# Mixer and mixture-of-experts layer on one core: where each expert's branch count is loaded into a register

## The chip, the cores and the metric

One core of one Trainium2 chip. The metric is the device time of one execution in microseconds (us). The kernel before takes 1189.96 us, the median of 3 runs (1186.68 to 1193.52).

## What is computed

A decoder layer on 256 tokens of width 1024: two kinds of attention, a gated merge and an output projection, and behind them a mixture of 32 experts, of which each token uses four. The change lies in the experts. Cut to them, the reference is:

```python
logits = (hf @ w_router + b_router).astype(jnp.float32)
top_val, top_idx = lax.top_k(logits, TOP_K)
top_w = jax.nn.softmax(top_val, axis=-1)
combine = ...
for e in range(N_EXPERTS):
    gu = hf @ w_gate_up[e] + b_gate_up[e]
    gate = jnp.minimum(gu[:, :D_EXPERT], SWIGLU_LIMIT)
    up = jnp.clip(gu[:, D_EXPERT:], -SWIGLU_LIMIT, SWIGLU_LIMIT)
    act = (up + 1.0) * (gate * jax.nn.sigmoid(SWIGLU_ALPHA * gate))
    y = y + combine[:, e:e + 1] * (act @ w_down[e] + b_down[e])
```

All weights are float32: 8 MiB of gate and up and 4 MiB of down per expert.

## The kernel before

The mixer and the router fill the first 235 us of the span. Then the loop over the experts runs (L1267), one **block** per expert `j`. A block multiplies up to 64 tokens that chose expert `j`, gathered to 64 rows, with the gate and up weights (`up_mm`, L1021, tile `ps_g`), and then does the down product of the expert ahead of it (`down(j - 1)`, L1089, tile `ps_d`), with the transposes of the activation (L1042, `ps_t`) between. Blocks with an odd `j` also add two finished experts to the output (`add_pair`, L1135), and every fourth gathers the tokens of the next four experts (L984).

**Weights.** They arrive in pieces of 2 MiB, four of gate and up and two of down per expert, all issued from the SyncE queue (SP, L78) in a fixed order. Ten slots hold them. `Slots.pump` sends a piece off once the piece that had its slot ten places earlier has been used, which is told by the matmuls that read it. A late block so delays transfers as well.

**Branches.** An expert may have more than 64 tokens. So a block begins, for `j` from 2 to 31, with `more(j)` (L1204): a branch on `arm[j]`, an integer that is over 0 where expert `j` or `j - 1` has tokens beyond 64. Where it is 0, as for nearly all, the body (`more_down`, `more_up`) is jumped over. The branch is on TensorE, VectorE, ScalarE and GpSimd, and each needs the number in a register. `load(arm, j)` (L1177, L1178) puts it there. On TensorE that is three instructions, which the trace calls TENSOR_LOAD, FUSED_REGOPS and SEQ_ASSERT (the first stands as TENSOR_LOAD, the others as ISA in the order of instructions below); they run in the engine's sequencer, which hands the matmuls to the engine. `hint(j + 1)` (L1200) puts a prefetch hint for the next block's branch behind the first matmuls of a block.

`arm` is computed once, in `counts()` (L924), during block 1. Nothing but that ties a load to a place in the program, and the scheduler, which orders each engine's instructions, puts the loads of TensorE into two bunches: 9 at the end of block 1, ahead of the branch of block 2, and 21 at the end of block 2, ahead of the branch of block 3. On VectorE and ScalarE each load stands at its own branch; GpSimd has none of the work here.

Of the kernel before, what the change touches and what calls it, by code (L numbers as in the profile page):

```python
# [100 lines left out]
def hybrid_layer(ctx: ExitStack, tc: tile.TileContext, x, c, w_mod, b_mod, g_pre_mix, g_post_mix,  # L101
# [118 lines left out]
    arm = keep.tile([1, E + 1], I32, name="arm")  # L220
# [9 lines left out]
    state_act = {}  # L230
# [776 lines left out]
    def gu_banks(n=2):  # L1007
        return [psg.tile([128, 512], FT, name="ps_g", tag=f"g{b}") for b in range(n)]

    def up_mm(e, C, xe, release=False, pg=None, ks=range(NK)):  # L1010

        n = 128 // C
        nb = 4 // n
        if pg is None:
            pg = gu_banks(nb)
        for k in ks:
            wt = W.get(i_gu[e][k // 2])
            for b in range(nb):
                for s in range(n):
                    c0 = s * nb * 512 + b * 512  # L1020
                    last = mm(pg[b][s * C:(s + 1) * C, :], xe[:, k, :], wt[:, k % 2, c0:c0 + 512],  # L1021
                              start=(k == 0), stop=(k == NK - 1), skip_group_check=True)
                    if k == ks[0]:
                        state_act["up"] = last
                    state_act["up_end"] = last
            if release and k % 2:
                W.done(i_gu[e][k // 2])
        return pg

    def up_out(pg, b, tag, bufs):  # L1030
        gu = wk.tile([128, 512], FT, name="gu", tag=tag, bufs=bufs)
        if b % 2:
            nc.vector.tensor_copy(gu, pg[b])  # L1033
        else:
            nc.scalar.copy(gu, pg[b])  # L1035
        return gu
# [40 lines left out]
    def down_mm(e, C, act, first=0, release=False, then=None):  # L1077

        nj = C // 8
        if e == E - 1 and first:  # L1080
            pds = gu_banks()
        else:
            pds = [pst.tile([128, 512], FT, name="ps_d", tag="t")] * 2
        for k in range(NK):
            wt = W.get(i_dn[e][k // 4])
            a = act[:, k % nj, (k // nj) * C:(k // nj) * C + C]
            for h in range(2):
                p0 = 64 * (h ^ first)
                mm(pds[h][p0:p0 + C, :], a, wt[:, k % 4, h * 512:(h + 1) * 512],  # L1089
                   start=(k == 0), stop=(k == NK - 1), skip_group_check=True)  # L1090
            if release and k % 4 == 3:
                W.done(i_dn[e][k // 4])
            if then and k % 4 == 3:
                then(k // 4)
        return pds
# [6 lines left out]
    def down(e, release=True, then=None):  # L1102

        pds = down_mm(e, 64, acts[e], e % 2, release, then)
        if e % 2 == 0:
            dns[e // 2] = pairs.tile([128, 2, 2, 512], FR, name="dn2", tag="dn")
        for h in range(2):
            rows = slice(64 * (h ^ (e % 2)), 64 * (h ^ (e % 2)) + 64)
            hi, lo = (dns[e // 2][rows, h, a, :] for a in range(2))
            weight = wsl[e // 2][rows, h:h + 1]  # L1110
            state_act["down"] = nc.scalar.activation(hi, pds[h][rows, :], AF.Copy, scale=weight)  # L1111
            nc.vector.scalar_tensor_tensor(lo, pds[h][rows, :], weight, hi.bitcast(FT), op0=OP.mult, op1=OP.subtract)  # L1112
# [52 lines left out]
    def more_down(e):  # L1165
        s0, C = CHUNKS[0]
        scatter(down_32(e, ov, "guo"), scatter_rows(e, s0, "so", C))

    def more_up(e):
        s0, C = CHUNKS[0]  # L1170
        for bank in gu_banks():
            nc.tensor.transpose(bank[:, :128], ident, ident)
        xo = gather([e], s0, C, "xo")[:, :, 0, :]
        pg = up_mm(e, C, xo, pg=[pst.tile([128, 512], FT, name="ps_go", tag="t")])
        up_act(e, C, 0, up_out(pg, 0, "guo", 1), ov)

    def load(t, j):  # L1177
        return nc.values_load(t[0:1, j:j + 1], engines=ENGINES, min_val=0, max_val=S)  # L1178

    def rest(e, i):  # L1180

        s0, C = CHUNKS[i]
        with tc.If(load(cnt, e) > s0):
            xo = gather([e], s0, C, "xo")[:, :, 0, :]
            pg = [pst.tile([128, 512], FT, name="ps_go", tag="t") for _ in range(C // 32)]
            for half in range(2):
                for q in range(2):
                    W.again(i_gu[e][2 * half + q], free_slots[q])
                up_mm(e, C, xo, False, pg, range(4 * half, 4 * half + 4))
            for q in range(2):  # L1190
                W.again(i_dn[e][q], free_slots[q])
            a = wk.tile([128, C // 8, 64], FT, name="ao", tag="xo")
            for b in range(C // 32):
                up_act(e, C, b, up_out(pg, b, "guo", 1), a)
            st = scatter_rows(e, s0, "so", C)
            scatter(down_64(e, a) if C == 64 else down_32(e, a, "guo"), st)
            if i + 1 < len(CHUNKS):
                rest(e, i + 1)

    def hint(j):  # L1200

        tc.mark_branch_hint_location(f"more{j}", "LikelyTaken", ENGINES[:1])

    def more(j):  # L1204


        with tc.If(load(arm, j) > 0, label=f"more{j}"):  # L1207
            if j - 1 not in FREE:
                with tc.If(load(cnt, j - 1) > 64):
                    more_down(j - 1)  # L1210
            if j < E - 1:
                with tc.If(load(cnt, j) > 64):
                    more_up(j)
            else:
                for bank in gu_banks():
                    nc.tensor.transpose(bank[:, :128], ident, ident)
                with tc.If(load(arm, E) > 0):
                    streamed = dict(W.tiles)
                    for e in range(E):
                        rest(e, int(e not in FREE))  # L1220
                    W.tiles = streamed

    last_slots = [W.items[k][2] for k in i_gu[E - 1]]
    free_slots = [W.items[k][2] for k in i_dn[E - 3]]
    quads, gus, acts, sts, wsl, dns = {}, {}, {}, {}, {}, {}

    def gather_quad(j, between=None):
        quads[j // 4] = gather([j, j + 1, j + 2, j + 3], 0, 64, "xe", between)

    def activate(j, b):  # L1230
        if b == 0:
            acts[j] = wk.tile([128, 8, 64], FT, name="act", tag="act", bufs=2)
        up_act(j, 64, b, gus[j][b], acts[j])
# [3 lines left out]
    def before_last():  # L1237

        add_pair((E - 4) // 2)
        scatter_pair(E - 2)  # L1240
# [26 lines left out]
    for j in range(E):  # L1267
        if j == 0:
            gather_quad(0, first_up)
        elif j not in FREE or j == E - 1:  # L1270
            if j == E - 1:
                before_last()
            more(j)
        xe = quads[j // 4][:, :, j % 4, :]
        if j == 0:
            pg = up_mm(0, 64, xe, True, pgs, range(NK - 2, NK))
        elif 1 < j < E - 1:
            pg = up_mm(j, 64, xe, True)
        elif j > 1:
            pg = up_mm(j, 64, xe, True, None, range(NK - 2))  # L1280
            with tc.issue_after(state_act["up_end"].ins):
                gate_row()
            up_mm(j, 64, xe, True, pg, range(NK - 2, NK))
        else:
            pg = gu_banks()
            for b, ks in enumerate((range(0, 4), range(4, 6), range(6, NK))):
                up_mm(1, 64, xe, True, pg, ks)
                if b < 2:
                    with tc.issue_after(state_act["up_end"].ins):
                        activate(0, b)  # L1290
        gus[j] = [up_out(pg, b, "gu", 2) for b in range(2)]
        if 0 < j < E - 1:
            with tc.issue_after(state_act["up"].ins):
                hint(j + 1)
        if j % 2 and 3 <= j < E - 1:
            with tc.issue_after(state_act["up_end"].ins):
                add_pair((j - 3) // 2)
        if j % 4 == 3 and j < E - 1:
            gather_quad(j + 1)
        if j == E - 1:  # L1300
            residual()
        if j == 0:
            weights()
        if j == 1:
            with tc.issue_after(state_act["up_end"].ins):
                counts()
                scatter_bias()
        if j % 2 and j < E - 1:
            scatter_pair(j - 1)
        if j:  # L1310
            down(j - 1, then=lambda b: activate(j, b))
    with tc.issue_after(state_act["down"].ins), tc.issue_after(state_act["sig"].ins):
        nc.scalar.preload_act_table_set(EXP_LN)
    down(E - 1)
# [44 lines left out]
```

## Time and profile before

| what | value |
|---|---|
| median of 3 runs | 1189.96 us |
| the profiled execution's own time | 1186.46 us |
| its span in the trace | 1184.7 us |
| TensorE matmul busy (PE) | 1060.4 us, 90% |
| TensorE weight load busy (PEld) | 536.6 us, 45% |
| VectorE (DVE), ScalarE (ACT), GpSimd (POOL) busy | 37%, 21%, 2% |
| moved by DMA | 461.60 MB, mean 390 GB/s |
| granted TensorE clock, mean | 0.973 |

The span is the time from the first to the last instruction; 1.8 us of the execution lie around it. The profiled execution is faster than all three timed runs, by 3.5 us than their median. "Idle before" a matmul tells what released it: `PEq L1207` is TensorE's own sequencer at the branch of `more`. A busy TensorE alone doesn't tell what sets the pace, since an engine that is fed at the pace of the transfers can look nearly as busy.

### The profile page before, as it was taken

Reading aid. Unit: us, or ns where it says so; the run is one execution under the profiler, and the core shown is the slowest. Engines: PE = TensorE matmul, PEld = TensorE weight load, DVE = VectorE, ACT = ScalarE, POOL = GpSimd, SP = SyncE. Lnnn points to the kernel's source line nnn. Section 1 sums busy time; section 2 is a strip of 40 time slices with the busy share of each in tenths; the row PEclk is TensorE's granted clock in tenths of the full one; section 3 lists DMA queues with packets and bytes.
Section 4 is the critical chain, followed back from the end, with each engine's and each line's share of the span. In section 5 each row is a group of like instructions: output and inputs, shape, how many; then the busy total and the mean of one; then the engine's idle time right before and its main releaser. Section 6 shows DMA issues by size and latency. Waiting matters only on the chain. (4 is left out here: it accounts for less than half of the span.)

```text
span 1184.7 us, 14417 instructions
## 1 busy us (share of the span) xinstructions
PE 1060.4 (90%) x5662; PEld 536.6 (45%) x5662; DVE 443.8 (37%) x963; ACT 248.2 (21%) x472; POOL 24.0 (2%) x39
## 2 busy tenths in 40 slices
PE   5999999898778999998999999899888988898886
PEld 4987999632233434344434343344323332333232
DVE  3586978614212333222323332223222322232234
ACT  3455674511000111011111111011001100010023
POOL 2022000000000000000000000000000000000000
PEclk9999999988989999997999999999999999999998
DMA  9988796979978999999999999999999999999993
GB/s 326 392 307 320 280 333 250 387 297 403 380 326 349 426 427 426 426 427 428 428 426 427 425 425 429 425 428 423 427 427 425 429 425 426 425 428 425 428 421 153
DMA packets 51902, 461.60 MB, mean 390 GB/s; under 512 B 4117, under 2 KB 4234, under 8 KB 27210
## 3 DMA queue, kind: packets, MB, share of 16 engines
q1 hardware_dynamic: 50992, 458.77, 93.7%
q8 instruction: 77, 1.26, 0.4%
q0 software_dynamic: 352, 0.67, 0.3%
q10 hardware_dynamic: 442, 0.58, 0.1%
q14 instruction: 39, 0.32, 0.1%
HBM read 458.96 MB, written 1.05 MB: 388 GB/s over the span
## 5 line engine op out<-in xcount | busy, mean ns | idle before, releaser
L1021 PE MATMUL ps_g<-w,xe 128*64 128x512 f32 x2048 | 465.2, 607 | 67.7 <-PEq L1207 34.0
L1021 PEld LDWEIGHTS ps_g<-w,xe 128*64 128x64 f32 x2048 | 161.8, 139 | 346.1 <-issue 245.7
L1089 PE MATMUL ps_d<-w,act 128*64 128x512 f32 x992 | 228.1, 601 | 12.4 <-DMA w<-in_w_down_dram 10.3
L1033 DVE COPY gu<-ps_g 128x512 f32<-128x512 f32 x32 | 22.1, 691 | 367.2 <-PE ps_g L1021 367.2
L1089 PEld LDWEIGHTS ps_d<-w,act 128*64 128x64 f32 x992 | 70.0, 138 | 135.3 <-issue 123.5
L1035 ACT COPY gu<-ps_g 128x512 f32<-128x512 f32 x32 | 18.7, 585 | 396.1 <-PE ps_g L1021 396.1
L1049 DVE TENSOR_TENSOR gate<-ps_t,bcol 128x256 f32<-128x256 f32 x64 | 27.1, 424 | 188.5 <-PE ps_t L1042 145.5
L481 PE MATMUL ps_p<-hT,whi 128*128 128x256 f32 x512 | 96.2, 287 | 1.6 <-DVE hT L422 1.6
L481 PEld LDWEIGHTS ps_p<-hT,whi 128*128 128x128 f32 x512 | 79.8, 191 | 5.2 <-issue 2.7
L431 DVE TENSOR_TENSOR wlo<-w,whi 128x1024 fp32r<-128x1024 f32 x56 | 68.6, 1227 | 30.4 <-ACT whi L430 29.2
L1058 ACT ACTIVATE act<-gate 128x256 f32<-128x256 f32 x64 | 26.6, 416 | 244.3 <-DVE gate L1057 244.3
L430 ACT CAST whi<-w 128x1024 fp32r<-128x1024 f32 x56 | 58.7, 1048 | 69.4 <-PE ps_p L481 25.0
L481 PE MATMUL ps_p<-hT,wlo 128*128 128x256 f32 x256 | 72.4, 285 | 0.0
L1042 PEld LDWEIGHTS ps_t<-ident,gu 128*128 128x128 f32 x260 | 36.3, 209 | 53.6 <-issue 51.9
L1111 ACT ACTIVATE dn<-ps_d,wsl 64x512 fp32r<-64x512 f32 x62 | 42.3, 682 | 85.9 <-PE ps_d L1089 70.3
L984 PE MATMUL ps_x<-p,xn 128*128 128x256 f32 (+1 forms) x288 | 43.1, 302 | 7.2 <-DVE p L975 3.2
L1042 PE MATMUL ps_t<-ident,gu 128*128 128x128 f32 x260 | 48.7, 310 | 0.8 <-ACT gu L1035 0.8
L481 PEld LDWEIGHTS ps_p<-hT,wlo 128*128 128x128 f32 x256 | 48.8, 191 | 0.9 <-DVE wlo L431 0.6
L1112 DVE SCALAR_TENSOR_TENSOR dn<-ps_d,wsl,dn 64x512 fp32r<-64x512 f32 x62 | 46.4, 748 | 1.5
L984 PEld LDWEIGHTS ps_x<-p,xn 128*128 128x128 f32 x288 | 40.2, 211 | 12.3 <-ACT xe L960 4.3
L1135 PE MATMUL y<-dn,st 128*128 128x512 f32 x128 | 35.3, 413 | 2.1 <-DVE dn L1112 1.2
L270 DVE SCALAR_TENSOR_TENSOR mod_acc<-w,sg,mod_acc 128x1024 f32<-128x1024 f32 x28 | 36.1, 1290 | 0.2
(264 smaller groups left out, 768.5 us busy)
## 6 DMA issues: line engine op xcount, KB each, us to landing
w<-in_w_gate_up_dram SPq DMA_DIRECT2D x128, 2048.0 KB, 32.9
w<-in_w_down_dram SPq DMA_DIRECT2D x62, 2048.0 KB, 29.8
w<-in_w_in_dram SPq DMA_DIRECT2D x8, 2048.0 KB, 8.0
w<-in_w_mod_dram SPq DMA_DIRECT2D x8, 2048.0 KB
w<-in_w_mod_dram SPq DMA_DIRECT2D x4, 1024.0 KB, 9.1
w<-in_w_mod_dram SPq DMA_DIRECT2D x8, 512.0 KB, 11.1
w<-in_w_in_dram SPq DMA_DIRECT2D x8, 512.0 KB
w<-in_w_out_dram SPq DMA_DIRECT2D x2, 2048.0 KB
```

Of the source, the lines that this page charges most:

```text
L270: nc.vector.scalar_tensor_tensor(self.acc, wt, sg[:, k:k + 1], self.acc, op0=OP.mult, op1=OP.add)
L430: state_act["whi"] = nc.scalar.copy(hi, w)
L431: nc.vector.tensor_tensor(lo, w, hi.bitcast(FT), op=OP.subtract)
L481: mm(ps[:, f % 2, :], w[:, kk, f * 128:(f + 1) * 128], hT[:, a, k, :], start=(k == 0 and i == 0 and f % 2 == 0), stop=(k == NK - 1 and i = ...
L984: mm(px[:, j, :], xn[:, t, a, sorted_feature(k0 + j)], p[:, t].rearrange("p a b -> p (a b)"), start=(t == 0 and a == 0), stop=(t == 1 and ...
L1021: last = mm(pg[b][s * C:(s + 1) * C, :], xe[:, k, :], wt[:, k % 2, c0:c0 + 512], start=(k == 0), stop=(k == NK - 1), skip_group_check=True)
L1042: nc.tensor.transpose(pt[:, j, :], gu[:, j:j + 509:4], ident)
L1049: nc.vector.tensor_tensor(dst, pt[:, :, 64 * m:64 * m + 64], bcol[:, b0 + 4 * b:b0 + 4 * b + 4, None].to_broadcast([128, 4, 64]), op=OP.add)
L1089: mm(pds[h][p0:p0 + C, :], a, wt[:, k % 4, h * 512:(h + 1) * 512], start=(k == 0), stop=(k == NK - 1), skip_group_check=True)
L1111: state_act["down"] = nc.scalar.activation(hi, pds[h][rows, :], AF.Copy, scale=weight)
L1112: nc.vector.scalar_tensor_tensor(lo, pds[h][rows, :], weight, hi.bitcast(FT), op0=OP.mult, op1=OP.subtract)
L1135: mm(yps[t][h], sts[p][:, h, t * 128:(t + 1) * 128], dns[p][:, h, a, :], start=False, stop=False, skip_group_check=True)
```

## The change

Each branch of `more(j)` uses a register that was loaded earlier, `flags[j]`. The load for `j + 1` is written in block `j`, tied behind that block's first matmuls on TensorE (`state_act["up"]`); the load for block 2 is written at the end of block 1, tied behind a ScalarE activation (`state_act["sig"]`). The loads of `cnt` inside the branches stay as they are.

```diff
     def more(j):
...
-        with tc.If(load(arm, j) > 0, label=f"more{j}"):
+        with tc.If(flags[j] > 0, label=f"more{j}"):
...
-    quads, gus, acts, sts, wsl, dns = {}, {}, {}, {}, {}, {}
+    quads, gus, acts, sts, wsl, dns, flags = {}, {}, {}, {}, {}, {}, {}
...
         if 0 < j < E - 1:
             with tc.issue_after(state_act["up"].ins):
                 hint(j + 1)
+                if j > 1:
+                    flags[j + 1] = load(arm, j + 1)
...
         if j:
             down(j - 1, then=lambda b: activate(j, b))
+        if j == 1:
+            with tc.issue_after(state_act["sig"].ins):
+                flags[2] = load(arm, 2)
```

In the built programs the order on VectorE, ScalarE, GpSimd and SyncE is the same before and after; TensorE's alone differs.

On TensorE, at the end of block 1 and ahead of the branch of block 2, there stood before, with seven more of the pairs TENSOR_LOAD and ISA x2 where the dots are:

```order
L1089 MATMUL ps_d<-w_2551,act 64x512 x8
L1042 MATMUL ps_t<-ident,gu 128x128 x4
L1178 TENSOR_LOAD arm
L1178 ISA x2
...
L1207 COMPARE_AND_BRANCH
```

Now one such pair stands there, so 8 of the 9 loads have moved on.

On TensorE, in block 2 and ahead of the branch of block 3, the difference is (the dots stand for 20 more removed pairs):

```order
 L1021 MATMUL ps_g<-w_2668,xe 64x512 x8
+L1178 TENSOR_LOAD arm
+L1178 ISA x2
 L1089 MATMUL ps_d<-w_2696,act 64x512 x8
 L1042 MATMUL ps_t<-ident,gu 128x128 x4
 L1089 MATMUL ps_d<-w_2706,act 64x512 x8
 L1042 MATMUL ps_t<-ident,gu 128x128 x4
-L1178 TENSOR_LOAD arm
-L1178 ISA x2
...
 L1207 COMPARE_AND_BRANCH
```

All 21 loads at the branch are gone, and one stands between the gate and up product and the down product of the block. Each of the blocks 3 to 30 has one at the same place; the total, 30 of them, is as before.

## Rows read from the trace of the kernel before

**Rows 1.** The page, 40 slices of 29.6 us: granted clock and transfer rate.

```profile
PEclk9999999988989999997999999999999999999998
...
GB/s 326 392 307 320 280 333 250 387 297 403 380 326 349 426 427 426 426 427 428 428 426 427 425 425 429 425 428 423 427 427 425 429 425 426 425 428 425 428 421 153
```

**Rows 2.** Busy time by stretch; the last three columns are clock, DMA share, GB/s.

```profile
core 0: us, PE busy (x) PEld busy (x) DVE busy (x) ACT busy (x) POOL busy (x), PEclk, DMA share, GB/s
280.00:290.00 10.00, 10.00 (x39) 3.33 (x37) 3.30 (x8) 0.42 (x1) 0.00 (x0) 0.78 0.98 391
290.00:390.00 100.00, 79.90 (x361) 32.44 (x360) 23.79 (x59) 10.85 (x20) 0.00 (x0) 0.90 0.88 356
330.00:340.00 10.00, 9.14 (x32) 3.24 (x34) 1.43 (x6) 0.00 (x0) 0.00 (x0) 0.72 0.38 121
390.00:780.00 390.00, 369.77 (x1786) 160.65 (x1786) 118.34 (x301) 48.91 (x90) 0.00 (x0) 0.98 1.01 426
780.00:1140.00 360.00, 308.67 (x1428) 120.70 (x1428) 103.11 (x259) 41.24 (x74) 0.00 (x0) 1.00 1.01 427
```

**Rows 3.** TensorE's waits from 780 to 1141 us: total us, times, longest.

```profile
PE ps_g L1021 <- DMA w<-in_w_gate_up_dram: 32.6, 30, 1.6
PE ps_d L1089 <- DMA w<-in_w_down_dram: 10.3, 12, 1.3
```

**Rows 4.** Page, issued transfers of gate and up: count, size, us to landing.

```profile
w<-in_w_gate_up_dram SPq DMA_DIRECT2D x128, 2048.0 KB, 32.9
```

**Rows 5.** TensorE in order of time: start, us, operation, idle before it and releaser.

```profile
294.98 15.42 PE L1021 MATMUL ps_g<-w,xe 128*64 128x512 f32 x64 [4.03 <-PEq L1207]
...
318.03 0.75 PE L1042 MATMUL ps_t<-ident,gu 128*128 128x128 f32 x4
330.86 16.25 PE L1021 MATMUL ps_g<-w,xe 128*64 128x512 f32 x64 [12.08 <-PEq L1207]
...
366.50 15.50 PE L1021 MATMUL ps_g<-w,xe 128*64 128x512 f32 x64 [3.14 <-PEq L1207]
...
390.83 13.95 PE L1021 MATMUL ps_g<-w,xe 128*64 128x512 f32 x64 [0.45 <-PEq L1207]
...
492.48 13.95 PE L1021 MATMUL ps_g<-w,xe 128*64 128x512 f32 x64 [0.45 <-PEq L1207]
...
602.37 13.95 PE L1021 MATMUL ps_g<-w,xe 128*64 128x512 f32 x64 [0.82 <-PEq L1212]
...
755.53 15.55 PE L1021 MATMUL ps_g<-w,xe 128*64 128x512 f32 x64 [3.75 <-PEq L1207]
...
1141.27 12.10 PE L1021 MATMUL ps_g<-w,xe 128*64 128x512 f32 x48 [2.92 <-PEq L1207]
```

**Rows 6.** Line 1178 on TensorE's sequencer, 284 to 300, then 300 to 332 us.

```profile
L1178 PEldq TENSOR_LOAD <-arm x9: 299/305/497, 287.7 to 293.4; - x9
...
L1178 PEldq TENSOR_LOAD <-arm x21: 297/299/318, 315.5 to 329.4; - x21
L1178 PEldq FUSED_REGOPS  x21: 146/146/146, 315.9 to 329.8; - x21
```

**Rows 7.** SyncE's queue: its issues in order of time, and its wait, 320 to 345.

```profile
307.00 11.47 SPq L78 DMA_DIRECT2D w<-in_w_gate_up_dram  x4
336.84 3.76 SPq L78 DMA_DIRECT2D w<-in_w_down_dram  x2
...
SPq L78 <- PE ps_g L1021: 24.3, 3, 18.3
```

**Rows 8.** Line 1207 on TensorE's sequencer: the branches of blocks 4 and 9.

```profile
L1207 PEldq COMPARE_BRANCH  x1: 5912/5912/5912, 360.1 to 360.1; - x1
...
L1207 PEldq COMPARE_BRANCH  x1: 328/328/328, 488.8 to 488.8; - x1
```

## The prediction

> **What bounds the kernel now.** I read the page's slices first: from slice 13 on the transfers hold 425 to 428 GB/s to the end, but at the start of the experts three slices in a row show 380, 326 and 349 [rows 1]. So transfers look like the limit of the experts, with something wrong at their start. The busy times by stretch say it closer: 426 and 427 GB/s over 390 to 1140 us, but 356 over 290 to 390, and as little as 121 in the ten us from 330 [rows 2].
>
> Then I asked whether TensorE or the transfers set the pace. TensorE's own pace is read where no wait for a weight stands: block 5 starts at 390.83 and block 9 at 492.48 [rows 5], so four blocks take 101.65 us, 25.4 each. An expert's weights are six pieces of 2048 KB [rows 4], 12.58 MB, and at 427 GB/s [rows 2] that is 29.5 us. Transfers are the slower of the two. TensorE only starts out behind them, catches up 4 us per block, and from 780 us on waits for weights, 32.6 + 10.3 us in all [rows 3]; from 390 to 780 the same view lists no such wait. From 390 us to the last block the transfers never pause, so the end of the kernel follows the end of the transfers. **A TensorE stall counts only where it makes the transfers pause**, and they pause only between 280 and 390 us.
>
> Why they pause there is in the order of time. TensorE stands idle for 4.03 us ahead of block 2, 12.08 ahead of block 3 and 3.14 ahead of block 4, each time released by its own sequencer at the branch; a normal block has 0.45 there [rows 5]. In the first two cases the sequencer is at the register loads: 9 from 287.7 us, 21 from 315.5 with the last begun at 329.4 [rows 6], which is 13.9 us for 20 of them, 0.69 us each (0.299 the load, 0.146 the register operation, the rest between). Meanwhile SyncE's queue has all slots full: it issues its last piece at about 318.5 (four from 307.00 in 11.47 us), then nothing until 336.84, waiting 18.3 us for block 3's first matmuls [rows 7]. That is the gap of 121 GB/s.
>
> **The change part by part.**
>
> *What is removed.* 8 of 9 loads ahead of block 2 and all 21 ahead of block 3. What is left there is a load (0.69) and a branch (0.33 [rows 8]), which begin while TensorE still has work queued: at block 3's bunch the first load starts at 315.5 [rows 6] and the engine works until 318.03 + 0.75 = 318.78 [rows 5], a lead of 3.3 us; at block 9 the branch is decided at 489.1 [rows 8] and the matmuls behind it start at 492.48. So both idle times should fall to 0.45: 3.58 + 11.63 = 15.2 us. The matmuls behind an idle time also ran slower, at a granted clock of 0.72 in the stretch from 330 [rows 2], partly its lower level of 1.2 GHz and partly 2.4, after the engine had stood idle: the same 64 took 15.42 and 16.25 where 13.95 is normal [rows 5], 1.47 + 2.30 = 3.8 us more. TensorE gets to block 4 some 19 us earlier.
>
> *What is added.* One load in each block, 0.69 us of the sequencer, behind the gate and up product. The cover is the sequencer's lead, 2.9 to 3.3 us, and the two down products that follow give it time to run ahead again before the branch. I cost it at nothing. Without cover it is 0.69 us per block, a pace of 26.1 against 29.5 for the transfers, and 2.1 us of the 19 by block 4: still nothing at the end, as the next step shows.
>
> *Nothing else moves.* Branches, hints and matmuls are the same in number; no wait is added on other engines. But the instructions ahead of each branch become fewer by up to 84 (28 loads of three), which shifts what lies in which block of fetched code. The trace shows that this can matter: the branch of block 4 took 5.91 us where block 9's took 0.33 [rows 8], 3.14 us of it exposed, and block 18 has a like gap of 3.75 [rows 5]. I can't tell from the trace which branches will be so after the change. Such a **late branch** costs 2.7 to 3.3 us idle and 1.6 us of slow matmuls, 4.2 to 4.9 in all.
>
> *What reaches the end.* TensorE's 19 us don't; the transfers' pauses do. From 290 to 390 us they move 356 GB/s where they can do 427 [rows 2]: (427 - 356) / 427 x 100 = 16.6 us of transfer missing. The ten us before lack another 0.8 (391). A little stays: block 2 can't give back its slots before block 1's down product is done, so I leave the 0.8 and 0.6 more in place and take **16.0 us**. With TensorE 19 us ahead at block 4, and 4 us gained per block after, it stays ahead even with the late branch there: the freed slots come faster than transfers fill them. What TensorE gains beyond that comes back as waits for weights, of which there will be more than now. Bounds: none of it if the pauses have another cause; at most 16.6 + 0.8 = 17.4, and 4.1 more if the branch of block 31 (idle 2.92 and as slow behind it [rows 5]), at the tail, should no longer be late.
>
> Against the profiled execution: 1186.46 - 16.0 = 1170.5 us. It is 3.5 us under the median of the runs, so against that 1189.96 - 16.0 = **1174 us**, the forecast.
>
> **The rivals.**
>
> *Late branches at the start.* Blocks 2 and 3 were never late before, perhaps only because the loads gave the fetch time. If blocks 2, 3 and 4 all are, at 4.9 us each, then of the 19 + 4.2 = 23.2 us that could go at most (block 4's lateness counted) 23.2 - 14.7 = 8.5 remain, and as TensorE's slots still set the transfers there, the gain is 8.5: 1181.5 us. For it: the shifted code. Against: the hint stands 20 us ahead of each branch, and 27 of the 30 blocks have no exposed wait of this kind.
>
> The Trainium skill has a rule that speaks for this rival and the one below ("Runtime: NRT & Kernel Launch", section "Instruction fetch mechanics"): a taken branch whose target lies outside the fetched window has to wait for a fetch, so every jump over a body should stall. The trace agrees in a few blocks only (5.91 us against 0.33 [rows 8]), perhaps because of the hints. By the rule alone all blocks would be late, which is the next rival's time.
>
> *Slower: late branches everywhere.* A block that comes to its branch without the pause may find the code not there, in all of 2 to 30. TensorE's pace becomes 25.4 + 4.9 = 30.3 us, more than the 29.5 of the transfers, and TensorE the bound. From 291.4 (294.98 - 3.58), 29 blocks of 30.3 and 33 for the two bodies that run (block 9 at 492.48 to block 12 at 602.37 [rows 5] is 109.9, less three of 25.4) bring block 31 to 1203 instead of 1141.27: about 1250 us. It decides where the extra time per block passes 2.8 us: 291.4 + 29 x 25.4 + 33 = 1061, and (1141 - 1061) / 29. That is more than half of all branches late; two of 29 are now.
>
> *The pauses are not TensorE's.* Then the end stays, at 1190. Against it stands the wait of 18.3 us by name [rows 7].
>
> *The loads stay bunched* in spite of the code: 1190 too. The instruction order speaks against it.
>
> **How the numbers follow.** Forecast 81%, late at the start 10%, pauses of another cause 5%, late everywhere 3%, still bunched 1%. About 0.5%, 6 us, is what a measurement here can tell from no change, so faster means under 1184. The forecast and most of the second case (8 of 10) are faster: 0.89. The rest of the second and the two cases without effect: 0.08. Slower: 0.03. The range goes from 1189.96 - 17.4 - 4.1 = 1168.5 to 1182, which takes in the first rival; 9% and the noise lie outside.
>
> **What would show it.** Right: idle before blocks 2 and 3 of about 0.45 us; single loads some 25 us apart on TensorE's sequencer; 290 to 390 us near 425 GB/s; the first waits for weights before 780 us and more than 43 us of them in total. Wrong: a rate under 400 in that stretch with the loads gone, branches of several us at blocks 2 to 4, or no more waits for weights than now.

## The result and the profile after

The changed kernel takes **1175.65 us**, the median of 4 runs (1173.67 to 1176.26), beside 1188.6 for the kernel before; the ratio is 0.9882, 95% interval 0.9848 to 0.9916. The forecast was 1174, the range 1168.5 to 1182. The profiled execution took 1175.85 us where that of before took 1186.46, a gain of 10.6. Of all executions in this study one, in the second measurement of the changed kernel, took 5381 us; it moves the median there by 0.1 us and is left out of the ratio.

The page's slices of 29.4 us, to be held against [rows 1]: the three weak slices at the start of the experts (380, 326, 349) are gone.

```profile
GB/s 325 391 297 319 294 317 265 370 295 414 419 427 425 428 426 425 426 426 428 428 426 427 425 427 425 428 426 427 426 426 426 426 427 426 427 427 425 428 404 106
```

The busy times by stretch answer to [rows 2]; the last column is GB/s. From 290 to 390 us there are 424 instead of 356, and 433 in the ten us where there were 121. TensorE's granted clock is 1.00 in these two stretches, its upper level, 2.4 GHz, where TensorE now has no long idle time.

```profile
280.00:290.00 10.00, 10.00 (x37) 3.08 (x35) 3.30 (x8) 0.42 (x1) 0.00 (x0) 0.77 0.95 384
290.00:390.00 100.00, 97.13 (x464) 42.95 (x462) 30.73 (x77) 12.98 (x23) 0.00 (x0) 1.00 1.01 424
330.00:340.00 10.00, 9.14 (x57) 6.01 (x55) 4.13 (x8) 2.26 (x4) 0.00 (x0) 1.00 1.02 433
```

TensorE in order of time, against [rows 5]: the idle times ahead of blocks 2, 3 and 4 fell from 4.03, 12.08 and 3.14 us to 0.52, 0.45 and 0.45, and the 64 matmuls behind blocks 2 and 3 are back at 13.95 us. The last row is block 31: there the idle time grew from 2.92 to 5.62.

```profile
292.23 13.95 PE L1021 MATMUL ps_g<-w,xe 128*64 128x512 f32 x64 [0.52 <-PEq L1207]
...
315.01 13.95 PE L1021 MATMUL ps_g<-w,xe 128*64 128x512 f32 x64 [0.45 <-PEq L1207]
...
345.68 14.65 PE L1021 MATMUL ps_g<-w,xe 128*64 128x512 f32 x64 [0.45 <-PEq L1207]
...
1130.13 12.65 PE L1021 MATMUL ps_g<-w,xe 128*64 128x512 f32 x48 [5.62 <-PEq L1207]
```

On line 1178 the sequencer has one load ahead of block 2 and two in the 32 us behind it, 22.8 us apart, where [rows 6] had 9 and 21.

```profile
L1178 PEldq TENSOR_LOAD <-arm x1: 507/507/507, 288.4 to 288.4; - x1
...
L1178 PEldq TENSOR_LOAD <-arm x2: 316/317/318, 301.7 to 324.5; - x2
```

SyncE's queue, against [rows 7]: the last of the four pieces from 302.78 on goes out at 314.25, and the next follows at 318.69, 4.4 us behind instead of 18.4.

```profile
302.78 11.47 SPq L78 DMA_DIRECT2D w<-in_w_gate_up_dram  x4
318.69 3.76 SPq L78 DMA_DIRECT2D w<-in_w_down_dram  x2
```

TensorE's waits over the whole span, against [rows 3]: 34.5 + 10.4 us for weights where the stretch shown of before had 32.6 + 10.3, and the first of them at 515 us instead of behind 780.

```profile
PE ps_g L1021 <- DMA w<-in_w_gate_up_dram: 34.5, 31, 2.6
PE ps_g L1021 <- PEq L1207: 20.6, 22, 5.6
PE ps_d L1089 <- DMA w<-in_w_down_dram: 10.4, 16, 1.3
```

The 10.6 us between the two profiled executions can be cut into pieces at the first matmuls of blocks 0, 30 and 31:

| kernel | start to block 0 | block 0 to 30 | 30 to 31 | 31 to end |
|---|---|---|---|---|
| before | 238.4 | 866.6 | 36.2 | 43.4 |
| changed | 239.7 | 851.5 | 38.9 | 44.0 |
| gain | -1.3 | 15.1 | -2.7 | -0.6 |

So 15.1 us were gained where the prediction looked for them, 3.3 were given back at the last block, and 1.3 lie ahead of the experts, where nothing was changed (block 0 starts between 238.2 and 240.5 us in the twelve traces of this study).

### The profile page after: what moved, and what is told of

Read it like the earlier page. It is cut to its first block, busy times and chain, and to the rows that moved or that the text cites. A ratio compares the mean times of both kernels' runs of the same rounds, so it can differ in the third digit from the quotient of the medians.

```text
span 1174.1 us, 14417 instructions
## 1 busy us (share of the span) xinstructions
PE 1059.6 (90%) x5662; PEld 539.2 (46%) x5662; DVE 443.9 (38%) x963; ACT 248.4 (21%) x472; POOL 24.0 (2%) x39
## 5 line engine op out<-in xcount | busy, mean ns | idle before, releaser
L1021 PE MATMUL ps_g<-w,xe 128*64 128x512 f32 x2048 | 463.4, 605 | 57.5 <-DMA w<-in_w_gate_up_dram 34.5
L1089 PE MATMUL ps_d<-w,act 128*64 128x512 f32 x992 | 228.0, 600 | 12.5 <-DMA w<-in_w_down_dram 10.4
```

## The experiments

The theory on trial: *an idle time of TensorE costs what it makes the transfers pause, and nothing else*. Rival A: TensorE's idle time adds up directly. Rival B: the gain came from the code that shifted, not from the loads. All medians are read against the kernel before as it ran beside them (1191.5, 1191.2 and 1192.6 us).

**The same stall at four places.** Further loads on TensorE, whose values nothing uses, are put behind the transposes at the end of block `AT`:

```diff
+                state_act["tr"] = nc.tensor.transpose(pt[:, j, :], gu[:, j:j + 509:4], ident)
...
             down(j - 1, then=lambda b: activate(j, b))
+        if j == AT:
+            with tc.issue_after(state_act["tr"].ins):
+                for _ in range(N):
+                    nc.values_load(arm[0:1, 0:1], engines=ENGINES[:1], min_val=0, max_val=S)
```

*AT = 1, N = 8.*

> The changed kernel with 8 further loads on TensorE at the end of block 1, whose values nothing uses; 9 stand there, as before the change. Theory (only a pause of the transfers reaches the end): idle before block 2 about 4 us, and a replay of slots and transfers with the durations of the traces gives 3.7 us of new pause near 300 us, so 1179.3 us against 1175.65. Rival A (TensorE's idle time adds up directly): 3.6 idle and 1.5 of slow matmuls, 1180.8. Rival B (the gain came from the shifted code and its branches): no change, 1175.7.

Measured 1179.05 us, ratio 0.9896 (0.9858 to 0.9933). The idle time before block 2 is 4.06 us, as it was in the kernel before, and 290 to 390 us fall to 409 GB/s: (427 - 409) / 427 x 100 = 4.2 us of transfer missing against 0.7 in the changed kernel, 3.5 more where the theory said 3.7. But blocks 30 and 31 have late branches here (3.40 and 6.05 us idle), so the end does not tell the theory from rival A. The pause is the one that the theory expects; rival A is decided only by the run before block 21, below. One of the six executions took 1170.07 us, the other five 1178.82 to 1181.82.

*AT = 2, N = 20.*

> The changed kernel with 20 further loads on TensorE at the end of block 2; 20 stand there where 21 did before the change. Theory: idle before block 3 about 11.5 to 12 us, a pause of the transfers between 320 and 340 us, 12.5 us in the replay, 1188 us. Rival A: 11.6 idle and 2.3 of slow matmuls, 1189.6. Rival B: no change, 1175.7.

Measured 1176.72 us, 0.9884 (0.9844 to 0.9924). At first sight rival B: nothing came back. The trace says otherwise. TensorE in order of time and the busy times by stretch of this kernel:

```profile
324.53 16.93 PE L1021 MATMUL ps_g<-w,xe 128*64 128x512 f32 x64 [11.46 <-PEq L1320]
...
1131.09 10.52 PE L1021 MATMUL ps_g<-w,xe 128*64 128x512 f32 x48 [0.45 <-PEq L1207]
```

```profile
290.00:390.00 100.00, 86.34 (x402) 36.43 (x402) 28.74 (x73) 12.05 (x22) 0.00 (x0) 0.93 0.94 389
```

The stall is back (11.46 us) and so is a pause: (427 - 389) / 427 x 100 = 8.9 us, 8.2 more than in the changed kernel. The replay's 12.5 (a calculation, not a run) was too much, probably because TensorE has a few us in hand without the stall of block 2 ahead of it. And block 30 starts 6.7 us later after block 0 than in the changed kernel. What hid it is the last row: block 31 has 0.45 us of idle time here instead of 5.62. The 60 instructions more have moved its code, and its branch is on time.

*AT = 7, N = 20.*

> The same 20 further loads, but at the end of block 7. Theory: the idle time before block 8 is again 11.5 to 12 us; the transfers do not pause there, but TensorE then lacks the lead that it needs for the two branch bodies that run at blocks 11 and 12, so they pause behind 540 us; 12.5 us in the replay, 1188 us. If TensorE's lead of 4 us per block is worth more than the replay says, 1176 to 1182. Rival A: 1189.6, with the pause, if any, at block 8. Rival B: 1175.7.

Measured 1174.44 us, 0.9863 (0.9823 to 0.9902), again with block 31 on time. The busy times by stretch show where the stall (11.51 us, inside the first stretch) is paid:

```profile
450.00:480.00 30.00, 18.49 (x76) 6.60 (x74) 3.32 (x8) 2.37 (x4) 0.00 (x0) 0.77 1.01 426
...
570.00:600.00 30.00, 26.91 (x153) 13.12 (x151) 11.44 (x26) 5.42 (x10) 0.00 (x0) 1.00 0.91 372
600.00:630.00 30.00, 29.48 (x140) 11.83 (x138) 7.64 (x21) 2.79 (x5) 0.00 (x0) 1.00 0.88 364
```

The transfers run at 426 through the stall itself and pause 110 us later, behind the two branch bodies of blocks 11 and 12, by (427 - 372) / 427 x 30 + (427 - 364) / 427 x 30 = 8.3 us. Block 30 comes 6.4 us later after block 0 than in the changed kernel. The place is as the theory said, the size again less than the replay's 12.5.

*AT = 20, N = 20.*

> The same 20 further loads, at the end of block 20, where TensorE waits for weights. Theory: idle before block 21 of 11.5 to 12 us, all slots are then waiting for transfers that go on, no pause, 1175.7 us (within 1.5), and TensorE's waits for weights fall by some 14 us from 45. Rival A: 1189.6. Rival B: 1175.7 with the waits for weights unchanged.

Measured 1169.57 us, 0.9825 (0.9784 to 0.9866). TensorE in order of time and by stretch:

```profile
831.51 17.13 PE L1021 MATMUL ps_g<-w,xe 128*64 128x512 f32 x64 [10.86 <-PEq L1207]
...
1124.38 10.52 PE L1021 MATMUL ps_g<-w,xe 128*64 128x512 f32 x48 [0.45 <-PEq L1207]
```

```profile
810.00:840.00 30.00, 18.58 (x75) 6.63 (x73) 7.63 (x21) 2.78 (x5) 0.00 (x0) 0.77 1.01 427
```

A stall of 10.86 us with slow matmuls behind it, and the transfers don't notice: 427 GB/s. Block 30 starts 851.6 us after block 0, as in the changed kernel (851.5), and the waits for weights fell from 44.9 to 31.8 us. Rival A is out: the same stall cost 6 to 7 us at block 30 ahead of blocks 3 and 8, and nothing here. That the end is 6 us *earlier* no theory had foreseen; it is block 31 again.

**Which branches are late.** A second question, then: what makes the branch of block 31 take 5.89 us? Two ideas, and the rival of the prediction in which all are late, were tried on the hints.

```diff
+        if 0 < j < E - 1:
+            with tc.issue_after(state_act["up_end"].ins):
+                hint(j + 1)
         if j % 2 and 3 <= j < E - 1:
```

> The changed kernel with a second prefetch hint for the same branch, behind the gate and up product, some 14 us after the first. Theory C (a hint is lost when it meets a running fetch of code, as the first hint of blocks 7, 19 and 31 did, within 0.3 us of one): the second one catches them, no branch takes over 3 us, the idle time before block 31 falls from 5.62 to about 0.5, 5 us less: 1170.5 us. Rival D (a late branch is one with no border of code blocks between hint and branch, and the hint alone starts no fetch): 60 instructions or so more shift the borders, other branches are late, about as many as in the changed kernel (3 over 5 us), and the end moves by -5 to +2 us as block 31 is among them or not.

Measured 1168.17 us, 0.9815 (0.9772 to 0.9858): the best of all. But four branches still take about 6 us, those of blocks 7, 18, 19 and 30, so theory C falls. Block 31 is not among them; block 30 starts 3.69 us late and the transfers go on meanwhile.

With the same lines and the first hint taken out:

> The changed kernel with the one hint behind the gate and up product instead of behind its first matmuls; the number of instructions is the same, their places almost. Theory C: the hints of blocks 7, 19 and 31 no longer meet the fetch that runs at a block's start; as few late branches or fewer, not at the same blocks; 1170.5 to 1176. Rival D: with half the distance from hint to branch, fewer borders lie between, so about half of all branches are late; those behind block 13 are hidden by the waits for weights, those before cost pauses: 1176 to 1190.

Measured 1173.53 us, 0.9866 (0.9818 to 0.9913). Blocks 7, 19 and 31 are late, the same three as in the changed kernel, so the place of the hint doesn't decide it. Of D there remains that the code's place does; its "half of all branches" is wrong. Block 30 comes 2.4 us earlier after block 0 than in the changed kernel, and not because of late branches: from 280 to 290 us TensorE's granted clock is 1.00 here (0.77 in the changed kernel, a mean of the two levels), block 2 starts sooner, and the transfers hold 424 and 425 GB/s up to 300 us instead of 384 and 397.

Without any hint:

> The changed kernel without any hint. If the hints keep the branches on time: every branch 6 us late, 3.3 us idle and up to 1.6 of slow matmuls per block, a pace of 28.7 to 30.3 us against the 29.5 of the transfers, pauses from block 2 on; 35 to 60 us more, 1210 to 1235. This is the price of the rival of the prediction in which all branches are late. If the hints do nothing: as many late branches as now, 1170 to 1180.

Measured 1179.72 us, 0.9899 (0.9851 to 0.9947): only 4 us more than the changed kernel. What late branches cost here is again a pause: the transfers fall to 259 and 203 GB/s in the 20 us from 590, behind the branch bodies of blocks 11 and 12 (an inner branch, L1212, takes 5.26 us there), 9.2 us of transfer, and block 30 comes 6.8 us later after block 0. Eight branches take 5.8 us or more (blocks 6, 7, 13, 18, 19, 24, 25, 31) where the changed kernel has three. Four rows of TensorE in order of time, blocks 6 to 9:

```profile
399.11 16.70 PE L1021 MATMUL ps_g<-w,xe 128*64 128x512 f32 x64 [3.63 <-PEq L1207]
427.75 15.65 PE L1021 MATMUL ps_g<-w,xe 128*64 128x512 f32 x64 [3.56 <-PEq L1207]
460.10 13.95 PE L1021 MATMUL ps_g<-w,xe 128*64 128x512 f32 x64 [0.45 <-PEq L1207]
482.88 13.95 PE L1021 MATMUL ps_g<-w,xe 128*64 128x512 f32 x64 [0.45 <-PEq L1207]
```

Most branches are on time without a hint: of the other 22, three take 0.9 to 2.5 us and the rest under 0.5. Whether the five late ones more than in the changed kernel come of the missing hints, or of the code that moved by 30 instructions, isn't separated.

**What a late branch waits for.** The page of each run lists a DMA queue for instructions, q8, with 77 transfers of about 16 KB each in the changed kernel. In the twelve traces 85 branches of TensorE's sequencer take more than 0.7 us, and each of them ends 2.3 to 2.6 us after a transfer on q8 has started. Of these, 39 stand at the start of a block and take 5.8 us or more; there that transfer starts only 3.3 to 4.2 us into the branch, and in the shorter ones earlier. By this regularity a late branch waits for a piece of code; that q8 feeds TensorE is read from it alone. The rule of the Trainium skill ("Runtime: NRT & Kernel Launch", "Instruction fetch mechanics"), by which a taken branch whose target lies outside the fetched window waits for its code, fits these 85 branches. The prediction read the rule as one for every jump over a body; it speaks only of targets that lie outside, and the traces show a wait in 8 of 30 blocks at full length without hints and in 3 of 30 in the changed kernel.

**The change with equal tails.** To separate the two effects, the 20 loads at the end of block 20 were also put into the kernel before. At block 31 its code then lies where it lies in the changed kernel with those loads.

> The kernel before with the 20 further loads at the end of block 20, as in the run before block 21: the two bunches of the kernel before stay, and the code at block 31 lies exactly where it lies in that run, whose branch of block 31 came on time. Theory (a late branch of block 31 depends on where its code lies, and costs at the tail alone): that branch takes under 1 us here too, from block 30 to block 31 33.7 us instead of 36.2, so 2.5 us under the kernel before, 1188.5 against its 1191; the idle time before block 21 is hidden. Against the changed kernel with the same 20 loads the time is then the transfers' pause alone, 15 us more. Rival: lateness at the tail is chance from run to run, the branch is late here, 1191.

> The changed kernel once more, on the same chip as its neighbours. Theory: the same blocks late (7, 19, 31), 1175.7 us; 13 to 15 under the kernel before. Rival (late by chance): other blocks late than 7, 19 and 31.

> The changed kernel with the 20 further loads at the end of block 20 once more, beside the kernel before with the same loads. Theory: 1169.6 us, 6 under the changed kernel, of which 5.2 is the branch of block 31, and 15 to 18 under the kernel before with the same loads. Rival: no difference from the changed kernel.

Measured: 1187.16 us for the kernel before with the loads, 0.9962 (0.9947 to 0.9977); 1176.02 for the changed kernel again, 0.9868 (0.9845 to 0.9891), late at the blocks 7, 19 and 31 as before; 1169.94 for the changed kernel with the loads, 0.9818 (0.9801 to 0.9834). The branch of block 31 in the changed kernel, in the changed kernel with the loads, and in the kernel before with them (in ns, and its time):

```profile
L1207 PEldq COMPARE_BRANCH  x1: 5889/5889/5889, 1123.8 to 1123.8; - x1
```

```profile
L1207 PEldq COMPARE_BRANCH  x1: 451/451/451, 1123.5 to 1123.5; - x1
```

```profile
L1207 PEldq COMPARE_BRANCH  x1: 439/439/439, 1140.1 to 1140.1; - x1
```

The theory's 2.5 us for the kernel before came out as 4.5 by the ratio (2.7 to 6.3); the trace shows 2.3 of it between blocks 30 and 31 and doesn't account for the rest. The traced execution of the kernel before took 1186.46 us, 6 less than its median here, so it may not show all that the others spend. Which branches are late is not chance in these traces: the changed kernel is late at the same three blocks twice, with the 20 loads at blocks 7, 19 and 29 twice, and the kernel before with those loads is late at block 29 and on time at block 31 as well. How long a late branch takes does vary, 5.89 and 6.65 us at block 31 in the two traces of the changed kernel. With equal tails the change is worth 1187.16 - 1169.94 = **17.2 us** (16.4 in the profiled executions, 15.8 of it between blocks 0 and 30). Rival B so accounts for a few us at the tail and not for the gain.

| kernel | block 0 to 30 | 30 to 31 | median |
|---|---|---|---|
| changed, again | 851.8 | 39.7 | 1176.02 |
| 8 loads before block 2 | 857.3 | 37.4 | 1179.05 |
| 20 before block 3 | 858.2 | 34.1 | 1176.72 |
| 20 before block 8 | 857.9 | 33.8 | 1174.44 |
| 20 before block 21 | 851.6 | 33.7 | 1169.57 |
| hint twice | 854.0 | 30.6 | 1168.17 |
| hint late | 849.1 | 39.2 | 1173.53 |
| no hint | 858.3 | 38.9 | 1179.72 |
| before, with 20 before block 21 | 867.4 | 33.9 | 1187.16 |
| changed, with 20 before block 21, again | 851.6 | 33.8 | 1169.94 |

## Why the prediction was right

- *The transfers set the pace, and only their pauses count.* Shown: the same 20 loads cost 6.7 us at block 30 ahead of block 3, 6.4 ahead of block 8 (paid 110 us later) and 0.1 ahead of block 21.
- *The idle times fall to 0.45 us and TensorE gains 19 us by block 4.* Right: 0.52 and 0.45. From block 0 to block 5 it took 152.4 us before and 129.5 now, 23.0 less: the 19 and the late branch of block 4, which the prediction had put at 4.2 and couldn't place; it went, by luck.
- *The added loads cost nothing.* Right: 0.45 us before each normal block, with a load of 0.5 us or so per block ahead of it.
- *16.0 us of pauses reach the end.* The pause shrank by (424 - 356) / 427 x 100 = 15.9 us, and block 30 comes 15.1 us earlier after block 0. With equal tails the end moved by 17.2 in the medians. The two stalls put back one at a time bring 3.5 and 8.2 us of pause; no run of the changed kernel puts both back together, or the late branch of block 4. That this branch went was not needed: pieces issued at 318.7 and 356.9 us land 17.4 and 18.4 us later in the changed kernel, where one issued into an empty queue (at 336.84 in the kernel before) landed after 7.7, so the transfers had some 10 us of work in hand (an estimate), more than the 4.2 to 4.9 of a late branch. The 1.4 us that the prediction left in place were there, 1.7 by the rates of 384 and 397 GB/s from 280 to 300 us, but its reason, block 2 waiting for block 1's down product, is not: with the hint late the same order of products leaves 0.1 us, at a granted clock of 1.00 instead of 0.77 from 280 to 290.
- *Late branches.* The one-sided term. The prediction allowed the branch of block 31 to be no longer late (4.1 us more gain) and late branches at blocks 2 to 4 to eat the gain, but not that block 31's could become later still: 5.89 us instead of 3.19, 3.3 us at the end. Moved code is not the cause of that: all 30 loads stand ahead of block 31 in both kernels, and the traces have 11433 records of TensorE ahead of its branch in both. Its piece of code starts 0.6 us into the branch in the kernel before and 3.4 in the changed kernel, 2.8 us later, and the branch takes 2.7 longer; why it starts later isn't known. None came at blocks 2 to 4, so the first rival did not occur; blocks 7 and 19 became late and cost nothing, as the transfers did not pause there.
- *More than 43 us of waits for weights, the first before 780 us.* Right in kind: 44.9 us, from 515 us on. But they took only 2.0 us more than before: of the 23.0 us that TensorE was ahead at block 5, 17.6 were left at block 11, the late branch of block 7 having taken most of the rest, and 15.1 at block 30.
- *The slower rival, all branches late*, was priced at 1250 us. Its state could not be brought about: even without hints only 8 of 30 are late, and that costs 4 us.
- *The transfers hold 425 to 428 GB/s from slice 13 on.* Misread a little: the row [rows 1] goes from 423 to 429, with 421 and 153 in the last two slices. Nothing hangs on it.

In the two profiled executions the gain came out at 10.6 us instead of 16.0: 0.9 is missing between blocks 0 and 30, 3.3 went at block 31 and the tail, and 1.3 lie ahead of the experts. In the medians it was 13 in the first measurement and 15.7 by the ratio in the second, so that the tail's 3.3 us can't be told from the scatter there. That 1174 came so close to 1175.65 is in part luck: the 16.0 were taken off the median of three runs, 1189.96, and the kernel before had medians from 1188.6 to 1192.6 in this study.

What stays open: why the piece of code for some branches starts so late. Whether block 31 is late goes with the number of instructions ahead of its branch (late with none, 24 more or 30 fewer, on time with 30 or 60 more) and not with the place of the hint; a hint that meets a running fetch is not the cause. The number of branches that take over 5 us goes from none (20 loads before block 3) to eight (no hint).

## What to carry to other kernels

Ask of a stall first whether the slowest resource feels it: look for the stretch where its rate drops, and price the stall by what is missing there, not by its own length. A stall can also be paid later, when slack that it has used up is wanted. And an edit that changes the number of instructions moves all code behind it, as far as the place where the numbers are equal again: compare two kernels at an inner mark as well as at the end, or give both the same tail, before a few us are put down to the edit.

## What was not expected of the hardware

A register load that nothing waits for and whose value nothing uses made the kernel faster: 20 of them at the end of block 20 took 6 us off the changed kernel (1176.02 to 1169.94) and 5 off the kernel before (1192.55 to 1187.16). They moved the code of block 31's branch, which is on time with them; from block 30 to block 31 the traces show 5.9 us of the 6, and 2.3 of the 5. At the start of a block, most branches that jump over the body take 0.3 to 0.45 us of the sequencer. A late one takes up to 6.7, all of it until 2.3 to 2.6 us after a piece of code has started on the instruction queue. Of a branch of some 6 us, 2.7 to 3.8 show as idle time where the engine still has matmuls queued, and 5.6 to 6.4 at block 31.
